# Negated copies of high weights, made on GpSimd instead of ScalarE

## The chip, the cores and the metric

The kernel runs on one core of one Trainium2 chip. The metric is the time of one execution in microseconds (us). Before the change it is 2362.22 us, the median of three runs (2359.66 to 2363.74).

## The reference

Two layers of a transformer-like trunk are computed for 128 context tokens and 512 latent tokens with shared weights of width 1024. Each layer is a half-step SwiGLU feed-forward block, a mixer (attention, pooling and convolution heads between an input and an output projection), and a second half-step feed-forward block. All are wrapped in modulated RMS norms:

```python
def ffn_sublayer(x, mod, k, g, w_in, w_out):
    h = modulated_norm(x, mod, k, g)
    gt, up = jnp.split(h @ w_in, 2, axis=-1)
    return x + 0.5 * mod[:, None, 3 * k + 2] * ((jax.nn.silu(gt) * up) @ w_out)

def trunk_layer(...):
    x = ffn_sublayer(x, mod, 0, norm_g[0], w_ffn_in[0], w_ffn_out[0])
    h = modulated_norm(x, mod, 1, norm_g[1])
    q, k, v, u_pool, u_conv, bg, cg = jnp.split(h @ w_in, IN_SPLITS, axis=-1)
    ...
    y = jnp.concatenate([attn, pool, conv], axis=-1) @ w_out
    x = x + mod[:, None, 5] * y
    x = ffn_sublayer(x, mod, 2, norm_g[2], w_ffn_in[1], w_ffn_out[1])
    return x, k, v
```

The modulation vectors come from a product of a condition vector with `w_ada` (1024 x 9216 for each layer). All data is float32.

## The kernel before

Activations are held transposed, features on the 128 partitions and 640 tokens along the row, in two halves of 320 columns. A float32 product is made from three faster ones (`mm3`, L352 to L354): every operand is split into a high part (rounded to float32r) and a low part (the rest), and the three matmuls are high weight by high activation, high weight by low activation, low weight by high activation. So each weight tile of 128 x 1024 passes four steps before TensorE can finish with it:

1. SyncE issues a load into a `raw` buffer (five of them; `load_raw`, L181).
2. ScalarE (ACT) copies it, rounded, into a `wh` buffer (four of them; L170).
3. The low part `wl` (four buffers) is made. Where `split_w` is given an engine, one subtraction on that engine does it (L176). Where it is not (`eng is None`), ScalarE writes the negated high part into `wl` (L173), and GpSimd (POOL) issues a DMA that adds `raw` onto `wl` (L174), so that `wl` becomes `raw - wh`.
4. TensorE (PE) multiplies; the third matmul of each triple (L354) reads `wl`.

A `raw` buffer is free for the next load only when its last reader is done, which in the second form of step 3 is the accumulating DMA. The loads of `w_ada` (L150) use the same five buffers in the first feed-forward block, where VectorE (DVE) multiplies and sums them (L309, L311).

The form without an engine is used 96 times: for all weights of the input product in the first feed-forward block but the first two columns (40), for all weights of the two mixers (44), and for the first four weights of each of the other three feed-forward blocks (12, `ups_by_half`). Most weights of those three blocks use sums of weight blocks (`fast_weights`) and the subtraction on VectorE.

At the end of each block `last_product` computes the last part of the output product half by half, and the residual stream `x` (L518), its squares (ScalarE, L251) and their sum (VectorE, L252) follow tile by tile. Then come the sum over partitions (PE, L375), the inverse root (L361 to L364) and the modulated norm: `norm_tail` (L401, L416, L417) ahead of a mixer, `seven` (L480, L483, L473, L474) ahead of a feed-forward block. While these run, the first four weights of the next block pass the steps above, because their `wh` buffers come free one after the other as `last_product` ends. These places are called transitions below; there are five, at about 523, 743, 1216, 1677 and 1900 us.

Each engine executes its instructions in the order of its own queue. That order is fixed when the program is built, by a list scheduler that goes by the order of the code and by durations that it assumes. An instruction that waits holds all that are behind it on its engine.

Of the kernel before, what the change touches and what calls it, by code (L numbers as in the profile page):

```python
# [12 lines left out]
AF = mybir.ActivationFunctionType  # L13
# [83 lines left out]
def trunk_kernel(ctx: ExitStack, tc: tile.TileContext, i: dict, o: dict):  # L97
    nc = tc.nc
# [21 lines left out]
    def f32(ap):  # L120
        return ap.bitcast(F32)
# [42 lines left out]
    def split_w(raw, nk, width, eng=None):  # L164

        view = lambda t: t[:, : nk * width].rearrange("p (k c) -> p k c", k=nk)
        size, tag = (1024, "") if nk * width > 512 else (512, "s")
        h = view(whp.tile([P, size], F32R, tag="wh" + tag, name="wh", bufs=4 if tag == "" else 2))
        lo = view(wlp.tile([P, size], F32R, tag="wl" + tag, name="wl", bufs=4 if tag == "" else 2))
        nc.scalar.activation(h, raw, AF.Copy)  # L170
        if eng is None:

            nc.scalar.activation(lo, f32(h), AF.Copy, scale=-1.0)  # L173
            nc.gpsimd.dma_start(lo, raw, accum_op=ALU.add)  # L174
        else:
            eng.tensor_tensor(lo, raw, f32(h), op=ALU.subtract)  # L176
        return h, lo
# [9 lines left out]
    def load_w(loads, nk=KD, width=P):  # L187
        return split_w(*raw_w(loads, nk, width))

    def load_cols(src, c0, width=P, eng=None):  # L190
        return split_w(*load_raw(src, c0, width), eng)
# [364 lines left out]
    def ffn(l, f, n, hs, side, finish, nxt, first=None):  # L556
# [83 lines left out]
        def fast_weights(j):  # L640

            nk = KD // 2
            up, *_ = load_raw(w_in, DFF + j * P)
            gate, *_ = load_raw(w_in, j * P)
            a1, a2, d1, d2 = up[:, :nk, :], up[:, nk:, :], gate[:, :nk, :], gate[:, nk:, :]
            add = lambda out, x, y: nc.vector.tensor_tensor(out, x, y, op=ALU.add)
            view = lambda t: t.rearrange("p (k c) -> p k c", k=KD)
            one, two = view(sum_tile()), view(sum_tile())
            ups = split_w(up, KD, P, nc.vector)
            add(one[:, :nk, :], a1, d1)  # L650
            add(one[:, nk:, :], d1, d2)
            add(two[:, :nk, :], one[:, nk:, :], a1)
            add(two[:, nk:, :], two[:, :nk, :], a2)
            late = split_w(d2, nk, P, nc.vector)
            twos = split_w(two, KD, P, nc.vector)
            ones = split_w(one, KD, P, nc.vector)
            first = lambda w: (w[0][:, :nk, :], w[1][:, :nk, :])
            second = lambda w: (w[0][:, nk:, :], w[1][:, nk:, :])
            return {1: first(ups), 2: second(ups), 3: second(twos), 4: late, 5: second(ones), 6: first(twos), 7: first(ones)}
# [731 lines left out]
```

## Time and profile before

| | us |
|---|---|
| median of three runs | 2362.22 |
| the profiled execution | 2360.58 |
| its span on the core | 2358.8 |
| PE busy | 2298.7 (97%) |
| DVE busy | 1546.5 (66%) |
| ACT busy | 1057.9 (45%) |
| POOL busy | 118.7 (5%) |

A row of the timeline gives the start, the duration, the engine, the line, the operation and its tiles, how many like it are merged into it, and in brackets how long the engine sat idle before it and what ended that. The chain of work that ended last is followed back from the last instruction, at each step to what released it. PEclk is the granted clock of TensorE as a share of full speed, and the DMA share is the mean busy share of 16 DMA engines.

### The profile page before, as it was taken

How to read it: one execution, taken by the hardware profiler on the slowest of the kernel's cores; microseconds unless marked ns; L12 is line 12 of the kernel's file. 1: busy time of each engine (PE TensorE's matmuls, PEld its weight loads, DVE VectorE, ACT ScalarE, POOL GpSimd, SP SyncE). 2: the span in 40 equal slices, each digit the busy share in tenths (PEclk: the TensorE clock that was granted, in tenths of full speed). 3: DMA queues.
4: the chain of work that ended last, by engine and by line, in shares of the span. 5: the costliest groups of instructions: out<-in, count | busy, mean ns of one | idle time of the engine just before them, and what ended most of it. 6: DMA issues, size and time to landing. Idle time of an engine off the chain costs nothing.

```text
span 2358.8 us, 40820 instructions
## 1 busy us (share of the span) xinstructions
PE 2298.7 (97%) x16558; PEld 2217.3 (94%) x16558; DVE 1546.5 (66%) x3166; ACT 1057.9 (45%) x1861; POOL 118.7 (5%) x151
## 2 busy tenths in 40 slices
PE   7899999999999999999999999999999999999999
PEld 6899999998978899999999999999898789999999
DVE  5546675556766766666669575676658687666674
ACT  4423232335766634243446343443556674344351
POOL 2101010001200000000000000000111000000000
PEclk9999999999999999999999999999999999999999
DMA  8858596727533444453433334433475232322321
GB/s 274 207 143 232 161 258 169 199 63 159 133 87 81 126 132 136 117 160 101 152 90 119 115 113 119 126 102 114 99 151 127 55 72 80 106 72 86 89 81 45
DMA packets 355124, 297.90 MB, mean 126 GB/s; under 512 B 27288, under 2 KB 303096, under 8 KB 354936
## 3 DMA queue, kind: packets, MB, share of 16 engines
q1 hardware_dynamic: 340932, 244.88, 34.4%
q0 software_dynamic: 13824, 50.34, 11.8%
q8 instruction: 130, 2.13, 0.4%
q14 instruction: 58, 0.48, 0.1%
q10 hardware_dynamic: 180, 0.07, 0.0%
HBM read 242.04 MB, written 2.88 MB: 104 GB/s over the span
## 4 chain that ended last, share of the span: by engine, by line
PE 82%; DMA 7%; DVE 4%; issue 4%; ACT 3%; ACTq 0%; POOL 0%; SPq 0%; POOLq 0%; DVEq 0%
PE acc L352 21%; PE acc L353 20%; PE acc L354 20%; PE mis L354 3%; PE mis L353 3%; PE mis L352 3%; DMA raw<-in_w_ffn_in 3%; DMA wl<-raw 2%; PE mis L275 2%; PE po L352 1%; PE po L353 1%; PE po L354 1%; PE po L1100 1%; PE acc L1060 1%; PE mis L1111 1%
## 5 line engine op out<-in xcount | busy, mean ns | idle before, releaser
L352 PE MATMUL acc<-h,wh 128*128 128x320 f32 (+1 forms) x2784 | 871.8, 315 | 22.6 <-ACT h L416 5.4
L353 PE MATMUL acc<-h,wh 128*128 128x320 f32 (+1 forms) x2784 | 865.7, 312 | 6.4 <-DVE h L412 3.9
L354 PE MATMUL acc<-h,wl 128*128 128x320 f32 (+1 forms) x2784 | 863.3, 311 | 8.3 <-DMA wl<-raw 8.3
L170 ACT ACTIVATE wh<-raw 128x1024 fp32r<-128x1024 f32 (+2 forms) x332 | 305.1, 920 | 624.8 <-PE mis L353 287.6
L352 PEld LDWEIGHTS acc<-h,wh 128*128 128x128 f32 x2784 | 527.0, 190 | 38.5 <-issue 12.0
L354 PEld LDWEIGHTS acc<-h,wl 128*128 128x128 f32 x2784 | 527.4, 190 | 11.6 <-DMA wl<-raw 11.2
L353 PEld LDWEIGHTS acc<-h,wh 128*128 128x128 f32 x2784 | 527.7, 190 | 8.6 <-DVE h L412 4.1
L176 DVE TENSOR_TENSOR wl<-raw,wh 128x1024 fp32r<-128x1024 f32 (+2 forms) x234 | 227.8, 974 | 53.4 <-ACT wh L170 48.9
L352 PE MATMUL acc<-g,wh 128*128 128x320 f32 x832 | 258.2, 310 | 0.0
L353 PE MATMUL acc<-g,wh 128*128 128x320 f32 x832 | 258.0, 310 | 0.0
L354 PE MATMUL acc<-g,wl 128*128 128x320 f32 x832 | 257.3, 309 | 0.0
L170 ACT ACTIVATE wh<-sums 128x1024 fp32r<-128x1024 f32 x120 | 126.4, 1059 | 204.6 <-PE acc L353 93.0
L176 DVE TENSOR_TENSOR wl<-sums,wh 128x1024 fp32r<-128x1024 f32 x120 | 146.4, 1224 | 70.4 <-ACT wh L170 51.0
L518 DVE SCALAR_TENSOR_TENSOR x<-acc,gate,x 128x128 f32<-128x128 f32 (+1 forms) x352 | 125.2, 393 | 84.1 <-PE acc L354 82.5
L353 PE MATMUL mis<-g,wh 128*128 128x320 f32 x576 | 177.9, 309 | 0.0
L354 PE MATMUL mis<-g,wl 128*128 128x320 f32 x576 | 177.8, 309 | 0.0
L352 PE MATMUL mis<-g,wh 128*128 128x320 f32 x576 | 177.8, 309 | 0.0
L174 POOL DMA_DIRECT2D wl<-raw x96 | 84.3, 878 | 1714.3 <-DVE x L518 1030.9
L352 PEld LDWEIGHTS acc<-g,wh 128*128 128x128 f32 x832 | 156.3, 188 | 1.8 <-issue 1.6
L354 PEld LDWEIGHTS acc<-g,wl 128*128 128x128 f32 x832 | 156.4, 188 | 0.2
L353 PEld LDWEIGHTS acc<-g,wh 128*128 128x128 f32 x832 | 156.3, 188 | 0.3
L311 DVE SCALAR_TENSOR_TENSOR sums<-raw,c,sums 128x512 f32<-128x512 f32 x196 | 135.1, 744 | 27.5 <-DMA raw<-in_w_ada 27.4
(208 smaller groups left out, 3206.5 us busy)
## 6 DMA issues: line engine op xcount, KB each, us to landing
raw<-in_w_ffn_in SPq DMA_DIRECT2D x176, 512.0 KB, 4.3
raw<-in_w_ada SPq DMA_DIRECT2D x128, 512.0 KB, 5.8
wl<-raw POOLq DMA_DIRECT2D x96, 512.0 KB, 5.6
raw<-in_w_ffn_out SPq DMA_DIRECT2D x48, 512.0 KB, 4.8
raw<-in_w_ffn_out SPq DMA_DIRECT2D x64, 320.0 KB, 3.7
raw<-in_w_in SPq DMA_DIRECT2D x20, 512.0 KB, 5.4
adaw<-in_w_ada SPq DMA_DIRECT2D x16, 512.0 KB, 10.1
raw<-in_w_in SPq DMA_DIRECT2D x16, 256.0 KB, 6.5
```

Of the source, the lines that this page charges most:

```text
L170: nc.scalar.activation(h, raw, AF.Copy)
L174: nc.gpsimd.dma_start(lo, raw, accum_op=ALU.add)
L176: eng.tensor_tensor(lo, raw, f32(h), op=ALU.subtract)
L275: last = nc.tensor.matmul(ps[32 * g : 32 * g + 32, 0:P], c2[:, 2 * q + k, :], r[:, k, g * P : (g + 1) * P], start=(q + k == 0), stop=(q + ...
L311: nc.vector.scalar_tensor_tensor(part[:, j, :], r[:, k, :], c, part[:, j, :], op0=ALU.mult, op1=ALU.add)
L352: nc.tensor.matmul(out, wh, xh, start=start, stop=False, skip_group_check=onto)
L353: nc.tensor.matmul(out, wh, xl, start=False, stop=False, skip_group_check=onto)
L354: return nc.tensor.matmul(out, wl, xh, start=False, stop=stop, skip_group_check=onto)
L518: nc.vector.scalar_tensor_tensor(xT[t][:, s:e], ps[:, s - a : e - a], gates[l][n][:, t, j : j + 1], xT[t][:, s:e], op0=ALU.mult, op1=ALU.add,)
L1060: nc.tensor.matmul(ps[:, :w], qs[2 * c + m][:, g, self.qc], self.kk[x][:, g, :], start=(x == 0), stop=(x == 1),)
L1100: nc.tensor.matmul(po[g * HD : (g + 1) * HD, 0:256], self.vs[x][:, g * HD : (g + 1) * HD], pts[:, g * 256 : (g + 1) * 256], start=(x == 0) ...
L1111: nc.tensor.transpose(pt[:, (g * 2 + m) * P : (g * 2 + m + 1) * P], self.pr[m][:, g, x * P : (x + 1) * P], ident,)
```

## The change

In the form without an engine, the negated copy of the high part is made by GpSimd, with a multiplication of the tile by -1, and not by ScalarE. GpSimd then issues the accumulating DMA as before. All 96 uses change alike. Nothing else is edited.

```diff
         nc.scalar.activation(h, raw, AF.Copy)
         if eng is None:
 
-            nc.scalar.activation(lo, f32(h), AF.Copy, scale=-1.0)
+            nc.gpsimd.tensor_scalar_mul(lo, f32(h), -1.0)
             nc.gpsimd.dma_start(lo, raw, accum_op=ALU.add)
         else:
             eng.tensor_tensor(lo, raw, f32(h), op=ALU.subtract)
```

## Rows read from the trace of the kernel before

**Rows 1.** The page: span, and busy time, share and instructions by engine.

```profile
span 2358.8 us, 40820 instructions
PE 2298.7 (97%) x16558; PEld 2217.3 (94%) x16558; DVE 1546.5 (66%) x3166; ACT 1057.9 (45%) x1861; POOL 118.7 (5%) x151
```

**Rows 2.** The page: chain that ended last, shares of the span by engine.

```profile
PE 82%; DMA 7%; DVE 4%; issue 4%; ACT 3%; ACTq 0%; POOL 0%; SPq 0%; POOLq 0%; DVEq 0%
```

**Rows 3.** Waits of PE: who waited for whom, us in total, times, longest.

```profile
PE acc L354 <- DMA wl<-raw: 8.3, 9, 1.7
```

**Rows 4.** Groups of instructions by form: busy us, mean ns | idle before, releasers.

```profile
L173 ACT ACTIVATE wl<-wh 128x1024 fp32r<-128x1024 f32 x96 | 101.2, 1056 | 1.0
L176 POOL TENSOR_TENSOR wl<-raw,wh 128x1024 fp32r<-128x1024 f32 x2 | 4.8, 2404 | 18.9 <-ACT wh L170 18.9
```

**Rows 5.** Timeline of POOL: six memsets in a run.

```profile
534.01 3.96 POOL L853 MEMSET pool<- 128x672 f32 x6
```

**Rows 6.** Timelines of ACT, POOL and PE, 59 to 70 us.

```profile
59.67 1.06 ACT L170 ACTIVATE wh<-raw 128x1024 fp32r<-128x1024 f32 x1 [3.93 <-PE acc L353]
63.11 1.04 ACT L173 ACTIVATE wl<-wh 128x1024 fp32r<-128x1024 f32 x1
64.75 1.01 POOL L174 DMA_DIRECT2D wl<-raw  x1 [13.49 <-ACT g L155]
69.48 0.56 PE L354 MATMUL acc<-h,wl 128*128 128x320 f32 x2 [1.71 <-DMA wl<-raw]
```

**Rows 7.** Timelines of ACT, POOL and PE, 76 to 117 us.

```profile
76.15 1.06 ACT L170 ACTIVATE wh<-raw 128x1024 fp32r<-128x1024 f32 x1 [3.82 <-PE acc L353]
79.50 0.87 POOL L174 DMA_DIRECT2D wl<-raw  x1 [5.92 <-ACT wl L173]
95.65 1.06 ACT L170 ACTIVATE wh<-raw 128x1024 fp32r<-128x1024 f32 x1 [3.04 <-DMA raw<-in_w_ffn_in]
100.12 0.86 POOL L174 DMA_DIRECT2D wl<-raw  x1 [14.08 <-ACT wl L173]
116.96 0.64 PE L352 MATMUL acc<-h,wh 128*128 128x320 f32 x1 [3.30 <-ACT sg L585]
```

**Rows 8.** The chain that ended last, one piece of 56 to 125 us.

```profile
113.38 2.74 DVE sums L311 x4
```

**Rows 9.** Busy time by stretch: PE, PEld, DVE, ACT, POOL; then PEclk, DMA share, GB/s.

```profile
74.00:84.00 10.00, 10.00 (x70) 10.00 (x69) 1.02 (x4) 4.30 (x7) 0.87 (x1) 1.00 1.06 255
...
118.00:120.00 2.00, 2.00 (x9) 2.00 (x8) 0.00 (x0) 1.97 (x3) 0.87 (x1) 0.50 0.61 183
```

**Rows 10.** Timelines of ACT, POOL and PE, the transition at 1216 us.

```profile
1221.24 1.04 ACT L170 ACTIVATE wh<-raw 128x1024 fp32r<-128x1024 f32 x1
1224.47 1.04 ACT L173 ACTIVATE wl<-wh 128x1024 fp32r<-128x1024 f32 x1
1225.92 0.89 POOL L174 DMA_DIRECT2D wl<-raw  x1 [4.76 <-DVE full L480]
1240.05 0.41 PE L353 MATMUL acc<-h,wh 128*128 128x320 f32 x1 [1.90 <-DVE h L474]
```

**Rows 11.** Timelines of ACT and POOL, the transition at 523 us.

```profile
530.50 1.06 ACT L170 ACTIVATE wh<-raw 128x1024 fp32r<-128x1024 f32 x1 [0.56 <-PE acc L353]
533.27 0.86 POOL L174 DMA_DIRECT2D wl<-raw  x1 [2.66 <-ACT wl L173]
```

**Rows 12.** Timeline of ACT, the transition at 743 us.

```profile
767.51 0.63 ACT L170 ACTIVATE wh<-raw 128x512 fp32r<-128x512 f32 x1 [5.67 <-DMA raw<-in_w_ffn_in]
```

**Rows 13.** Timeline of DVE beside POOL subtractions, then beside POOL memsets.

```profile
19.76 6.64 DVE L401 SCALAR_TENSOR_TENSOR tmp<-x,gain,rr 128x128 f32<-128x128 f32 x8
...
536.35 0.93 DVE L401 SCALAR_TENSOR_TENSOR tmp<-x,gain,t 128x128 f32<-128x128 f32 x3
```

**Rows 14.** Busy time by stretch, the transition at 743 us.

```profile
743.00:760.00 17.00, 15.80 (x105) 15.07 (x103) 14.07 (x33) 16.15 (x31) 3.16 (x4) 1.00 0.61 125
```

## The prediction

> **What bounds the kernel now.** The page comes first: PE is busy for 2298.7 of 2358.8 us [rows 1], and the chain that ended last runs over PE for 82% [rows 2]. ACT, which the change relieves, is busy 45% of the span, so its busy time as a sum is worth nothing. Only the some 60 us in which PE does not work can shrink or grow, and the time at which its clock is low. So the second view is PE's waits: the third matmul of a triple waits for the accumulated low weights in nine places, 8.3 us together and 1.7 us at most [rows 3]. All nine lie between 60 and 120 us or in the five transitions; from 123 us to the end of that block, and through the long middle of the other blocks, PE hardly waits. So the change is worth what it does in these six places, and the third reading is the timelines there: when `wh` of a weight ends on ACT, when its accumulating DMA starts on POOL, and who waits for that.
>
> **What is removed and added.** ACT loses 96 copies of 1.056 us, 101 us in all [rows 4], POOL gains 96 multiplications. POOL has 118.7 us of work [rows 1] and waits most of the time, so its sum is no limit; the duration of one counts, since it stands in the path of each weight. No row shows a one-input multiplication of 128 x 1024 on POOL. From below: six memsets of 672 columns, which only write, take 3.96 us, 0.66 each [rows 5]; by columns that is 1.0 us for 1024. From above: the subtraction of the same size, which reads two tiles, takes 2.4 us [rows 4]. If writing costs 1.0, each of the two reads costs 0.7, and one read gives 1.0 (hidden under the write) to 1.7 (added to it). I take 1.3, nearer the memset, and keep 1.0 and 2.4 as ends. The Trainium skill ("GPSIMD Engine Reference", section 4.1 Engine selection) calls GpSimd roughly at line rate for one-input elementwise work; with its clock of 1.2 GHz that is, as an estimate, 0.85 us. By that alone the sum below would be 2 to 3 us better; no row before shows it.
>
> **The gap from `wh` to the DMA.** Where nothing disturbs it, the path is the end of `wh`, 1.06 us of copy, then 0.4 us from ACT to POOL (1224.47 + 1.04 to 1225.92 [rows 10]): 1.5 us at best. At 530.50 + 1.06 to 533.27 it is 1.7 [rows 11]. After the change it is the same hop of 0.4, 1.3 of multiplication, and a hand-over to the DMA behind it on POOL, which no row shows and I put at 0.2 (0 to 0.4): 1.9 us. So an undisturbed weight loses 0.2 to 0.4 us. But on ACT the copy stands in a queue with other work, and there the gap is much longer. POOL has next to nothing else to do. So the gain lies where the gap of before is well above 1.9.
>
> **Place 1, 60 to 123 us.** Three links follow one another on the chain that ended last. (a) `wh` ends at 60.73 and the copy starts only at 63.11, behind a table load and the activations of the two columns before; the DMA starts at 64.75 and PE waits for it until 69.48 [rows 6]. Gap 4.0, after it 1.9: 2.1 us earlier. The activations that stood behind the copy move up by 1 us as well, so the next `wh`, for which PE also waits, is no later than that. (b) `wh` ends at 77.21, DMA at 79.50 [rows 7]: 2.3 to 1.9, 0.4 earlier. Its landing frees a `raw` buffer for the load whose arrival starts the `wh` at 95.65. (c) That ends at 96.71, its DMA starts at 100.12 [rows 7], since activations that waited for DVE stood between: 3.4 to 1.9, 1.5 earlier. Its landing frees the buffer for a load of `w_ada`, for which DVE's sums at 113.38 wait [rows 8]; behind them stand the bias copies, then the activation that frees PSUM, and PE waits 3.30 us until 116.96 [rows 7]. Sum 4.0 us. SP issues these loads in its own order behind the DMAs' landings, so its queue moves with them. After that wait TensorE runs at 0.50 (1.2 GHz): 9 matmuls in 2 us where 70 in 10 us are usual [rows 9]. That lasts from 117 to some 122.4 us, 5.4 us at 4.5 in place of 7 matmuls per us, a loss of 2 us. The wait would shrink to some 1.4 us (3.30 less the 1.9 by which the end of the chain gains on PE), and I expect the clock to stay up: 2 us more. From there PE is busy without a break, so what is won stays.
>
> **Place 2, transition at 1216 us.** `wh` ends at 1222.28, the DMA starts at 1225.92, since five other pieces of ACT stood before the copy [rows 10]: 3.6 to 1.9, 1.7 us. This DMA frees the buffer for a load for which DVE's in-order queue waits with the norm behind it, up to PE's wait until 1240.05 [rows 10]. Gain 1.7 us.
>
> **The other four transitions.** The gap that decides is the 1.7 of [rows 11] or within 0.1 of it: 0.2 us later each, 0.8 us lost.
>
> **DVE.** The new instruction can hold DVE. Beside the two subtractions on POOL, eight DVE instructions took 6.64 us, 0.83 each; beside POOL's memsets three of the same shape took 0.93, 0.31 each [rows 13]. So POOL work that reads held DVE for 4 of its 4.8 us, work that only writes did not. The multiplication reads one tile. The ends are no hold and 1.3 us each. In the transition at 743 us DVE is idle for 2.9 of 17 us [rows 14], so four holds (5.2 us) push it by up to 2.3 us; but there ACT waits 5.67 us for a load behind all this [rows 12], which covers it. In the two transitions to a mixer a hold of the last addition of squares (up to 0.9 us) ends before the last low weights land. So I charge nothing for it, with up to 4 us (two uncovered pushes) kept for the range. The Trainium skill ("SBUF — State Buffer", section "Who interferes with whom") says that a VectorE instruction with two SBUF inputs contends with any GpSimd instruction that reads SBUF, and names no exception for one input: by it the full hold applies, which speaks against this change. The rows agree as far as they go. By the rule the 4 us are possible; without a hold the sum stays as it is.
>
> **The sum.** 4.0 + 2.0 + 1.7 - 0.8 = 6.9 us. The profiled execution took 2360.58 us, 1.8 more than its span, and becomes 2353.7. The median of the runs is 1.6 above it, so I predict 2355.
>
> **The rivals.** (R1) The waits close only partly. Between 74 and 84 us the DMA share is 1.06 [rows 9], and an earlier DMA into full queues may land no earlier. Then links b and c and the clock are lost and 2.1 + 1.7 - 0.8 = 3.0 remain: 2359 for the median, within 0.2%. For it speaks the share, against it that link c runs over queues and hand-overs, not bytes. (R2) Slower, by the multiplication itself. At its upper end of 2.4 us the gap is 3.0. Link a keeps 1.0, b loses 0.7, c keeps 0.4, 1216 keeps 0.6: 1.3 won, without the clock. The other four transitions lose 1.3 each, 5.2. Four holds are now 9.6 us against 2.9 idle at 743, 1.0 more than the 5.67 us of cover, and 1216 and 1900 are alike, 3 in all. Net 7 us slower: 2369. The gains and these prices balance near 1.9 us for one multiplication; from some 2.2 on it is slower by more than 0.2%. For it speaks the subtraction's 2.4, against it that only one tile is read. (R3) The build orders the queues anew. The scheduler goes by assumed durations, so an instruction may come to stand elsewhere. One bad place costs like the one at 767.51, 5.67 us on ACT [rows 12], of which PE sees 3 to 5; one good place gives as much. No row can say which. It widens the range on both sides.
>
> **How the numbers follow.** A measurement of this kernel can tell about 0.2%, 4.7 us, from no change. Forecast 0.50 (faster, 2355; with multiplications of 1.0 us, and the rest of the waits for low weights gone, down to 2347). R1 0.28, at 2359. R2 0.10, at 2369. R3 0.12, split evenly into 0.04 each for faster, same and slower. The uncovered holds move 0.02 from the forecast's faster to slower. Faster 0.50 + 0.04 - 0.02 = 0.52; same 0.28 + 0.04 = 0.32; slower 0.10 + 0.04 + 0.02 = 0.16. The range takes in the forecast's lower end and R1 with some loss, and reaches to just under R2: 2347 to 2368.
>
> **What would show it right or wrong.** Right: multiplications near 1.3 us on POOL, starting some 0.4 us behind `wh`; the DMA of link a near 62.6 us, that of link c some 4 us earlier; PE's wait near 117 us under 2 us and PEclk at full there; the wait near 1240 us earlier; nothing changed from 123 to 520 us but the shift. Wrong: multiplications of 2 us and more, DVE instructions of twice their length beside them, longer waits of PE for `wl` or for squares in the transitions, or another order of the queues with a new wait.

## The result and the profile after

The change makes the kernel slower: 2404.1 us (median of 4 runs, 2401.1 to 2405.72) against 2360.94 us for the kernel before on the same chip (4 runs), a ratio of 1.0177 with a 95% interval of 1.016 to 1.0194. The forecast was 2355, its range ended at 2368. The profiled execution has a span of 2403.9 us, against 2358.8 [rows 1].

The page after, with busy time by engine, then the chain that ended last by engine:

```profile
PE 2312.9 (96%) x16558; PEld 2229.9 (93%) x16558; DVE 1600.5 (67%) x3166; ACT 967.9 (40%) x1765; POOL 399.7 (17%) x247
PE 70%; issue 7%; DMA 5%; POOL 3%; DVE 2%; ACT 2%; SPq 0%; ACTq 0%; POOLq 0%; DVEq 0%
```

ACT lost 90 us and POOL gained 281, as the change says. But DVE, which the diff does not touch, gained 54 us with the same 3166 instructions, and POOL has come onto the chain. The other shares of the chain can't be laid beside [rows 2]: after the change it is followed back only to 255 us, and it opens there with 51 us of "issue", while the shares are still of the whole span. PE is busy for 14.2 us longer with the same 16558 matmuls: TensorE's granted clock is 0.983 in the mean of this execution, where it was 0.993. So some of the 45 us between the two spans are not waits but matmuls at the lower clock.

The costliest groups after, by form (busy us, mean ns | idle before and releasers): the new multiplication, the subtraction with two inputs beside it, and three groups of DVE whose code is unchanged.

```profile
L173 POOL TENSOR_SCALAR wl<-wh 128x1024 fp32r<-128x1024 f32 x96 | 286.1, 2980 | 1457.5 <-ACT wh L170 1429.2 <-ACT pts L1117 24.6 <-DMA out_new_k<-ko 3.7
L176 POOL TENSOR_TENSOR wl<-raw,wh 128x1024 fp32r<-128x1024 f32 x2 | 4.8, 2404 | 18.2 <-ACT wh L170 18.2
L252 DVE TENSOR_TENSOR ssq<-ssq,sq 128x320 f32<-128x320 f32 x70 | 45.2, 646 | 21.4 <-ACT sq L251 20.7
L309 DVE TENSOR_SCALAR sums<-raw,c 128x512 f32<-128x512 f32 x28 | 23.7, 872 | 14.4 <-DMA raw<-in_w_ada 14.3
L932 DVE TENSOR_TENSOR qw<-rope 128x512 f32<-128x512 f32 x8 | 9.4, 1177 | 0.6
```

One multiplication takes 2.98 us in the mean (2.76 to 5.76 over the 96, median 2.79). That is longer than the subtraction that reads two tiles, 2.40 here as in [rows 4], which the forecast had taken as its upper end. The three DVE groups had means of 489, 480 and 691 ns before.

Waits of PE after (us in total, times, longest):

```profile
PE acc L352 <- ACT h L473: 12.2, 4, 5.7
PE mis L375 <- DVE ssq L252: 9.5, 2, 4.8
PE acc L352 <- ACT sg L585: 8.2, 7, 2.7
PE acc L1060 <- DVE mx L1071: 7.4, 2, 4.2
PE acc L354 <- DMA wl<-raw: 6.5, 3, 4.4
PE acc L352 <- DVE u L1026: 5.5, 2, 2.8
```

The wait for the accumulated low weights, on which the forecast was built (8.3 us [rows 3]), has shrunk a little in total and is longer in its worst place. The loss is in other rows: norms and squares at the transitions, activations in the first block, the attention's scores. So the question is by which way a longer step on POOL reaches them, and where.

For that the two traces were laid over each other: the start of the n-th matmul of one kernel, less the start of the n-th matmul of the kernel before, at four marks (in us of the kernel before). The stretch to 135 us holds the forecast's place 1; the attention starts are 611 to 705 and 1759 to 1853 us. Each number is what a kernel lost (or won, negative) in that stretch, from one profiled execution each; the experiments of the next section stand in the same table. Single executions of the kernel before lie between 2355.0 and 2365.2 us, so a difference of 2 us in one stretch can be chance.

| kernel | to 135 | 135 to 513, rest of the first block | the two attention starts | all other | last matmul |
|---|---|---|---|---|---|
| after the change | -2.1 | 12.9 | 19.0 | 15.4 | 45.2 |
| e1, extra reads on POOL | -2.2 | 4.9 | 20.4 | 6.3 | 29.4 |
| e2, delay only | 1.8 | 7.3 | 2.4 | 6.5 | 18.0 |
| e5, POOL busy without reads | -0.4 | 6.3 | 2.7 | 1.7 | 10.3 |
| e6, a longer delay | 5.3 | 17.2 | 9.9 | 5.1 | 37.5 |
| e3, subtraction on POOL | -3.9 | 1.3 | 20.4 | 15.5 | 33.3 |
| e9, half on POOL, half on ACT | -2.4 | 0.7 | 13.6 | 9.6 | 21.5 |
| e4, change in the first block alone | -3.5 | 13.1 | 0.5 | -3.5 | 6.6 |
| e7, e3 in the first block alone | -6.1 | 1.3 | 1.1 | -1.0 | -4.7 |
| e8, subtraction on DVE there | -11.1 | -0.9 | 2.5 | 0.9 | -8.6 |
| e10, subtraction on DVE everywhere | -10.8 | -0.9 | 12.5 | -0.5 | 0.3 |

### The profile page after: what moved, and what is told of

It is laid out like the page before. It is cut to its first block, busy times and chain, and to the rows that moved or that the text cites. A ratio compares the mean times of both kernels' runs of the same rounds, so it can differ in the third digit from the quotient of the medians.

```text
span 2403.9 us, 40815 instructions
## 1 busy us (share of the span) xinstructions
PE 2312.9 (96%) x16558; PEld 2229.9 (93%) x16558; DVE 1600.5 (67%) x3166; ACT 967.9 (40%) x1765; POOL 399.7 (17%) x247
## 4 chain that ended last, share of the span: by engine, by line
PE 70%; issue 7%; DMA 5%; POOL 3%; DVE 2%; ACT 2%; SPq 0%; ACTq 0%; POOLq 0%; DVEq 0%
PE acc L352 18%; PE acc L354 17%; PE acc L353 17%; PE mis L354 3%; PE mis L353 3%; PE mis L352 3%; DMA raw<-in_w_ffn_in 3%; POOL wl L173 2%; DMA wl<-raw 2%; PE mis L275 1%; PE po L353 1%; PE po L354 1%; PE po L352 1%; PE po L1100 1%; PE acc L1060 1%
## 5 line engine op out<-in xcount | busy, mean ns | idle before, releaser
L352 PE MATMUL acc<-h,wh 128*128 128x320 f32 (+1 forms) x2784 | 875.2, 317 | 33.5 <-ACT h L473 12.2
L170 ACT ACTIVATE wh<-raw 128x1024 fp32r<-128x1024 f32 (+2 forms) x332 | 305.1, 919 | 668.4 <-PE mis L353 289.6
L173 POOL TENSOR_SCALAR wl<-wh 128x1024 fp32r<-128x1024 f32 x96 | 286.1, 2980 | 1457.5 <-ACT wh L170 1429.2
L170 ACT ACTIVATE wh<-sums 128x1024 fp32r<-128x1024 f32 x120 | 126.0, 1058 | 200.7 <-PE acc L353 91.8
```

The costliest lines, as they stand in the source:

```text
L173: nc.gpsimd.tensor_scalar_mul(lo, f32(h), -1.0)
L352: nc.tensor.matmul(out, wh, xh, start=start, stop=False, skip_group_check=onto)
```

## The experiments

Three theories stood at the start. T1: the way to the low weight is longer, so what waits for it, or for the `raw` buffer that it frees, comes later. T2: POOL's reads hold DVE. T3: the scheduler put the queues in another order, which costs by itself. A fourth, T4, came with the first results: POOL is busy for longer with each weight, so that the next weight's transfer waits in its queue.

To size T1, one figure is taken from each trace: for each of the 96 uses, the time from the end of ACT's activation that makes `wh` (L170) to the start of POOL's issue of the accumulating DMA (L174). Its median is 1.72 us before and 3.38 us after the change.

**e1, reads without a delay.** POOL does the reading beside the weight's own path.

```diff
             nc.scalar.activation(lo, f32(h), AF.Copy, scale=-1.0)
-            nc.gpsimd.dma_start(lo, raw, accum_op=ALU.add)
+            extra_negations(nc, tc, idle, f32(h), nc.gpsimd.dma_start(lo, raw, accum_op=ALU.add))
+def extra_negations(nc, tc, idle, h, last):
+    flat = h.rearrange("p k c -> p (k c)")
+    for c in (0, 480):
+        with tc.issue_after(last.ins):
+            last = nc.gpsimd.tensor_scalar_mul(idle, flat[:, c : c + 480], -1.0)
```

> The copy stays on ACT, as before; behind each accumulating transfer GpSimd makes two more multiplications of 480 columns of the same high weight into a scratch tile that nobody uses. The result is the same. So GpSimd reads about as much per weight (960 of 1024 columns, about 2.6 us by the 2.79 us that 1024 columns took after the change), but no low weight waits for these reads, unless the next weight's transfer is queued behind them. Theory T1 (the longer way to the low weight: 2.8 us instead of 1.06 us and a hand-over): between 2360 and 2372 us. Theory T2 (GpSimd's reads hold DVE): DVE's busy time goes up by about 45 us as it did after the change, and the time is 2385 us or more, most of the 43 us. Theory T3 (another order of the queues): 2360 to 2365 us, since the copy is where it was.

Measured: 2389.45 us, ratio 1.0118 (1.0094 to 1.0142), 28.8 us above before. DVE was busy for 1611.3 us. That is T2's number, for reads that nobody needs, with the copy where it was before. T3 has no part in it: in the trace of e1 the instructions of PE, DVE and ACT and the loads stand in the order of before. But the gap from `wh` to the DMA also grew a little, to 2.35 us, since a DMA can stand behind the extra reads; e5 takes that apart.

**e2, a delay without reads.** The fills write a scratch tile and read nothing; `seen` ties them behind ACT's copy.

```diff
-            nc.scalar.activation(lo, f32(h), AF.Copy, scale=-1.0)
-            nc.gpsimd.dma_start(lo, raw, accum_op=ALU.add)
+            seen = small.tile([P, 1], F32, tag="seen", name="seen", bufs=4); nc.scalar.activation(lo, f32(h), AF.Copy, scale=-1.0, accum_out=seen)
+            delayed(nc, tc, idle, seen, lambda: nc.gpsimd.dma_start(lo, raw, accum_op=ALU.add))
+def delayed(nc, tc, idle, seen, issue):
+    pause = nc.gpsimd.memset(seen, 0.0)
+    for _ in range(4):
+        ...
+            pause = nc.gpsimd.memset(idle, 0.0)
```

> The copy stays on ACT; between its end and the issue of the accumulating transfer GpSimd makes five fills of a scratch tile (one of 1 column, four of 200), which write and read nothing. By the fills in the trace of before this is about 1.8 us per weight; the result is the same. T1 (the longer way to the low weight): DVE's busy time stays within 10 us of before's 1546 us and the time is 2385 to 2405 us. T2 (reads hold DVE): 2361 to 2370 us. T3 (order): 2361 to 2365 us.

Measured: 2377.92 us, ratio 1.0068 (1.0048 to 1.0088), 17.3 us above before; DVE 1549.0 us, as before. The median gap is 3.29 us, nearly the 3.38 of the changed kernel, so this is about the price of the change's delay with DVE left free (425 matmuls, nearly all at the transitions, also come in another order). It lies between what T1 and T2 expected, so neither alone explains the change at the price that was put on it.

**e3, the shortest way on POOL.** One subtraction in place of copy and accumulating DMA.

```diff
-            nc.scalar.activation(lo, f32(h), AF.Copy, scale=-1.0)
-            nc.gpsimd.dma_start(lo, raw, accum_op=ALU.add)
+            nc.gpsimd.tensor_tensor(lo, raw, f32(h), op=ALU.subtract)
```

> The low weight is made by one subtraction on GpSimd, raw minus high, of 2.4 us; copy and accumulating transfer are both left out, the result is the same up to rounding. The low weight is ready 2.4 us and a hand-over after the high one, where it was about 8 us before and about 10 us after the change. T1 (the longer way): 2345 to 2362 us, no slower than before. T2 (reads hold DVE; here both operands are read, for 2.4 us per weight): DVE's busy time at least 35 us above before's, the time 2380 us or more, though the way to the low weight is the shortest of all. T3: not told apart.

Measured: 2396.2 us, ratio 1.0148 (1.0123 to 1.0173), as T2 expected. DVE was busy for 1677.7 us, 131 more than before. The table shows where each theory holds: in the first block, where the delay counted, the kernel is ahead (-3.9) or hardly behind (1.3); at the attention starts it loses 20.4 us, though its low weights are ready 2.4 us behind the high ones, where the adding transfer alone took 5.6 at the median before.

**e4, the change in the first block alone.**

```diff
+            (nc.gpsimd.tensor_scalar_mul(lo, f32(h), -1.0) if on_pool[0] else nc.scalar.activation(lo, f32(h), AF.Copy, scale=-1.0))
...
+        last = x == len(steps) - 1; on_pool[0] = x == 0
```

> The multiplication is on GpSimd in the first feed-forward block alone (40 of the 96 uses) and on ACT in the rest. By the drift of the matmul starts between the two traces the change had lost 10.8 us by the end of that block (2.1 won to 134 us, 12.9 lost from there): T1 and T2 both expect 2369 to 2374 us. T3 (the order of the whole program is rebuilt and costs by itself): the loss isn't where the edit is, so less than 5 us or more than 20 us.

Measured: 2370.95 us, ratio 1.0046 (1.0031 to 1.0061), 10.3 us above before, as expected from the drift. The loss of 13.1 us lies in the stretch where the edit is, and behind it nothing is lost. That is against T3, but not all of it, since the queues of the later blocks are those of before in e4. The order can be read from the traces: after the change 48 matmuls between 60 and 80 us and 500 at the transitions behind 705 us stand elsewhere than before, and none in the rest of the first block or at the attention starts. So PE's order does not explain the losses there. DVE's order is another in the first block, at 46 places behind 135 us; in e9 it is another at 29, with 0.7 us lost. What the new order costs at the transitions, inside the 15.4 us of "all other", no run shows.

**e5 and e6, POOL busy or late, without reads.** e5 is e1 with ten fills in place of the two reads; e6 is e2 with eight fills in place of four.

```diff
-            nc.gpsimd.dma_start(lo, raw, accum_op=ALU.add)
+            pauses(nc, tc, idle, nc.gpsimd.dma_start(lo, raw, accum_op=ALU.add), 10)
+def pauses(nc, tc, idle, last, n):
+    for _ in range(n):
+        with tc.issue_after(last.ins):
+            last = nc.gpsimd.memset(idle, 0.0)
```

> As in the run with extra reads, the copy stays on ACT and GpSimd is kept busy behind each accumulating transfer, but by ten fills of a scratch tile (200 columns, 0.28 us and 0.04 us between them in the run with the delay: 3.2 us), which read nothing. GpSimd's time per weight is then that of the run with extra reads (3.26 us behind a transfer of 0.92 us); the result is the same. If the 28.8 us of that run came from reads that hold DVE (T2): DVE stays within 10 us of before's 1546 us and the time is 2361 to 2368 us. If they came from GpSimd's queue being long (a theory T4: the next weight's transfer, and the loads behind it, start later): 2380 us or more.

Measured: 2369.73 us, ratio 1.0033 (1.002 to 1.0045), 9.4 us above before, just over what T2 alone expected and far from T4's 2380.

> As in the run with the delay, but with eight fills instead of four between ACT's copy and the transfer: about 2.7 us, the length of the multiplication in the changed kernel, with nothing read; the result is the same. The way to the low weight and GpSimd's time per weight are then both those of the changed kernel or a little longer, and only DVE is free. If delay and hold add up, and the delay is worth what is left of the 43 us (about 14 to 18 us for the 1.3 us of the earlier run, more here): 2380 to 2395 us. If the delay alone explains the change: 2400 us or more. If it were worth nothing beyond the earlier run: 2378 us.

Measured: 2396.78 us, ratio 1.0157 (1.0141 to 1.0174), 36.4 us above before, 1.8 over the range that was given. The delay turned out longer than meant: the median gap is 5.04 us, since ACT's 1.06 us stand ahead of the fills. So e6 overshoots the change's own delay and can't be compared with it directly. It gives a slope: 36.4 us for 3.32 us of delay, 11.0 us for each; e2 has 17.3 for 1.57, the same 11.0. POOL's longer queue is in both.

e1 against e5 is the clean pair for the reads. First e1, then e5: busy time, POOL's extra instructions, and the DVE group that shows it best.

```profile
PE 2310.3 (97%) x16558; PEld 2225.6 (93%) x16558; DVE 1611.3 (67%) x3166; ACT 1060.4 (44%) x1861; POOL 406.0 (17%) x343
L1397 POOL TENSOR_SCALAR idle<-wh 128x480 bf16<-128x480 f32 x192 | 312.9, 1629 | 7.9
L932 DVE TENSOR_TENSOR qw<-rope 128x512 f32<-128x512 f32 x8 | 7.5, 937 | 0.6
```

```profile
PE 2306.7 (97%) x16558; PEld 2222.8 (94%) x16558; DVE 1550.8 (65%) x3166; ACT 1057.3 (45%) x1861; POOL 378.7 (16%) x1111
L1396 POOL MEMSET idle<- 128x200 f32 x960 | 292.1, 304 | 49.6
L932 DVE TENSOR_TENSOR qw<-rope 128x512 f32<-128x512 f32 x8 | 5.5, 690 | 0.6
```

POOL spends as long per weight in both (3.3 and 3.6 us with the idle time between), and the gap from `wh` to the DMA is 2.35 and 2.25 us. What differs is the reads (and the number of instructions, two for ten), and they cost 19.7 us (2389.45 less 2369.73); the order of the queues is that of before in e5 too. With reads, L932 takes 937 ns in the mean; with fills 690, as before. By the table, 17.7 us of that lie at the attention starts (20.4 less 2.7).

So the experiments price three parts of the change: 17.3 us for the delay (e2), 9.4 for POOL's longer queue (e5), 19.7 for the held DVE (e1 less e5). They add to 46.4 where 43.2 were measured. They need not add exactly, since e2 has some of the longer queue in it and a hold beside a wait is hidden; e1 also held DVE for longer than the change does (60.5 us more busy time than e5, where the change has 54.0 more than before). Each part was measured in another kernel, so its size within the changed kernel is an estimate. By the table e1 and e2 together give 12.2 us in the rest of the first block, 22.8 at the attention starts and 12.8 elsewhere, where the change lost 12.9, 19.0 and 15.4.

**e7 and e8, the other way to the low weight, in the first block alone.** A subtraction in place of copy and accumulating DMA, for those 40 weights: on POOL in e7 (`nc.gpsimd`), on DVE in e8.

```diff
+        eng = eng or first[0]
...
+        last = x == len(steps) - 1; first[0] = nc.vector if x == 0 else None
```

> The low weight by one subtraction on GpSimd, without copy and accumulating transfer, in the first feed-forward block alone (40 of 96 uses); the rest as before. By the drift of the run that did it everywhere (2.6 us ahead of before at 513 us of before's time, all losses behind it): 2355 to 2360 us. A theory by which any hold of DVE costs where it happens: 2370 us or more.

> The same subtraction in the first block alone, but on DVE: about 1.1 us per weight of DVE's own time (two SBUF inputs, 1024 columns, by the 0.49 us for 320 and 0.74 us for 512 columns: up to 1.5 us), against 2.5 us that GpSimd's held it. If in this block the way to the low weight is what counts: 2353 to 2360 us. If DVE has no room there: 2365 us or more.

Measured: e7 2358.57 us, ratio 0.9997 (0.9987 to 1.0006), no difference, though DVE was busy for 57.9 us more (1604.4). So a hold does not cost its full length wherever it happens; the shorter way may hide some of its cost. e8 2352.39 us, ratio 0.9969 (0.9959 to 0.998), faster than both kernels, 0.6 below its range. DVE's subtraction took 1.22 us, and the 45 us of work that DVE gained (1591.8 for 1546.5 us) found room there. The same window of before and of e8 shows what was to be won (PE, PEld, DVE, ACT, POOL busy; then PEclk, DMA share, GB/s):

```profile
60.00:134.00 74.00, 65.83 (x427) 64.35 (x429) 31.64 (x68) 33.45 (x52) 9.67 (x11) 0.95 0.83 206
```

```profile
60.00:134.00 74.00, 74.00 (x513) 73.60 (x512) 54.87 (x101) 26.54 (x47) 0.00 (x0) 1.00 0.53 150
```

PE is never idle in e8 and its clock is at 1.00 (2.4 GHz) in the mean of the window, so 8.2 us of idle time and the slow stretches are both gone: 11.1 us by the drift.

**e9, the multiplication at the length that the forecast assumed.** POOL takes 512 columns, ACT the other 512.

```diff
-            nc.scalar.activation(lo, f32(h), AF.Copy, scale=-1.0)
+            (m := nk // 2, nc.scalar.activation(lo[:, m:], f32(h)[:, m:], AF.Copy, scale=-1.0), nc.gpsimd.tensor_scalar_mul(lo[:, :m], f32(h)[:, :m], -1.0))
```

> Each negated copy is shared: 512 of its 1024 columns on GpSimd (about 1.4 us by the 2.79 us of 1024), 512 on ACT (about 0.55 us), at the same time; the accumulating transfer follows both. The result is the same. So GpSimd's multiplication has about the length that the forecast assumed (1.3 us) and the transfer starts about as early after the high weight as before (1.5 to 1.9 us). By the forecast's own sum: 2351 to 2358 us. By the parts measured since (17.3 us for a transfer 1.6 us later, 9.4 us for GpSimd's queue at 3.2 us more per weight, 19.4 us for 3.3 us of reads): a transfer about 0.2 us later 2 us, queue 3 to 4 us, reads 8 to 9 us, so 2370 to 2378 us.

Measured: 2380.38 us, ratio 1.0086 (1.0071 to 1.0101), 20.6 us above before, 2.4 over the range of the parts and 22 over the forecast's sum. The multiplication took 1.48 us at the median, the gap 2.05. Of the 6.0 us that the forecast put on place 1 it won 2.4, with 0.7 lost in the rest of that block; at the attention starts, which the forecast left out, 13.6 us were lost.

**e10, subtraction on DVE for all 96.** `first[0]` is `nc.vector` throughout.

> The low weight by one subtraction on DVE (1.1 to 1.2 us) in all 96 uses, without copy and accumulating transfer. In the first block alone this brought the time to 2352 us. If DVE's own time is what the other places lack (at the attention starts and the changes between blocks PE waits for DVE), the 56 more uses cost more than they bring: 2356 to 2372 us. If the length of the way counts there too: 2345 to 2352 us.

Measured: 2356.39 us, ratio 0.999 (0.998 to 0.9999), no difference that counts. The 11 us of the first block come again and 12.5 us go at the attention starts, where PE waits for DVE (its wait for `u`, L1026, is 8.0 us in place of 1.3). That agrees with T2: there DVE's time seems to be short, whether its own work or a hold takes it. But 50 matmuls of each attention start also come in another order.

## Why the prediction failed, step by step

**What bounds the kernel.** That PE is the bound, and that only its waits and its clock can move, was right. The step that failed is "so the change is worth what it does in these six places". A stretch in which PE hardly waits was read as one in which there is slack. In the rest of the first block, where the forecast expected "nothing changed from 123 to 520 us but the shift", 12.9 us were lost. Pieces of the chain that ended last, after, from that stretch (start, us, what):

```profile
306.88 3.94 POOL wl L173
311.23 5.26 DMA wl<-raw
316.53 5.74 DMA raw<-in_w_ada
322.37 0.76 DVE sums L311
...
325.72 8.97 DMA raw<-in_w_ffn_in
334.80 1.06 ACT wh L170
```

The multiplication, 3.94 us long here, delays the landing, the landing frees a `raw` buffer, SP's queue stands for that buffer with the load of `w_ada` and the load of a weight behind it, and that weight's `wh` comes late. The forecast followed this very loop as link c, but only where PE already waited.

**The multiplication (1.3 us, bounds 1.0 and 2.4).** The term of the sum that was mis-sized: 2.79 at the median, above the upper end. Both steps behind it failed: that a read adds less than a write, and that one input can't take longer than two. The Trainium skill ("GPSIMD Engine Reference", section 4.1 Engine selection) calls one-input work roughly line-rate, which was estimated at 0.85 us; here it took more than three times that, and the measurement decides.

**The gap (1.9 us).** Timelines of ACT, POOL and PE after, 59 to 70 us, for link a:

```profile
59.04 1.06 ACT L170 ACTIVATE wh<-raw 128x1024 fp32r<-128x1024 f32 x1 [3.93 <-PE acc L353]
60.19 2.79 POOL L173 TENSOR_SCALAR wl<-wh 128x1024 fp32r<-128x1024 f32 x1 [9.57 <-ACT wh L170]
63.31 1.04 POOL L174 DMA_DIRECT2D wl<-raw  x1 [0.33 <-POOL wl L173]
68.08 0.64 PE L354 MATMUL acc<-h,wl 128*128 128x320 f32 x1 [3.27 <-DVE g L156]
```

The hop from ACT to POOL took 0.1, not 0.4, and the hand-over to the DMA 0.33, not 0.2; with 2.79 between them the gap is 3.2 us. Against 4.0 before [rows 6] link a kept 0.8 of its 2.1. Links b (78.75 to 81.97) and c (94.48 to 97.70) have the same 3.2: against 2.3 and 3.4 before [rows 7], b lost 0.9 and c won 0.2. That is nothing in sum. PE still waited, 3.27 us at 68 us (the DVE instruction named ended at 66.2; a transfer issued at 63.31 that takes 4.6 to 5.3, as in the chain above and below, lands then).

**Place 1 and the clock.** The kernel was 2.1 us ahead at 135 us all the same. This is no merit of the shorter path: e1, which keeps the copy on ACT and the order of all queues, is 2.2 ahead there too. e4, with the same edit in this place, is 3.5 ahead. Whether any of it is more than chance is not shown. The clock did not stay up; its slow stretches moved (windows after, columns as above):

```profile
68.00:72.00 4.00, 3.92 (x15) 3.92 (x16) 1.84 (x2) 0.96 (x2) 3.70 (x3) 0.50 0.85 138
100.00:110.00 10.00, 8.23 (x47) 8.24 (x48) 8.53 (x18) 2.97 (x6) 6.41 (x2) 0.83 0.91 264
```

At 68 to 72 us PE works at 1.2 GHz after a stretch with the wait of 3.27 us, as it did at 118 us before [rows 9] after a wait of 3.30 us [rows 7]. That this place holds a gain was right (6.0 with the clock were forecast, e8 won 11.1). It took a way to the low weight without a transfer.

**Transition at 1216 us (1.7 won).** Lost instead: 4.4 us between 1171 and 1341 us. A new wait of 4.39 us for a low weight stands there, and the chain of one weight after the other on POOL is behind it: 2.8 to 3.1 us of multiplication and 0.9 of issue give about 4 us per weight, four weights in a row.

```profile
1244.92 2.77 POOL L173 TENSOR_SCALAR wl<-wh 128x1024 fp32r<-128x1024 f32 x1 [458.70 <-ACT wh L170]
1248.09 0.90 POOL L174 DMA_DIRECT2D wl<-raw  x1 [0.41 <-DVE full L480]
1249.41 2.76 POOL L173 TENSOR_SCALAR wl<-wh 128x1024 fp32r<-128x1024 f32 x1 [0.42 <-ACT wh L170]
1252.58 0.92 POOL L174 DMA_DIRECT2D wl<-raw  x1 [0.41 <-POOL wl L173]
1259.58 0.64 PE L354 MATMUL acc<-h,wl 128*128 128x320 f32 x1 [4.39 <-DMA wl<-raw]
```

The forecast had called POOL free, "next to nothing else to do"; with one weight behind the other POOL's own next multiplication is what else it has to do.

**DVE (nothing charged, 4 us kept).** The second failed step, and by the prices above the larger. The hold exists, near the size that the forecast wrote down as an end (1.3 us) and then covered. Timelines of POOL, DVE and PE after, the first transition to a mixer:

```profile
536.44 1.37 DVE L252 TENSOR_TENSOR ssq<-ssq,sq 128x320 f32<-128x320 f32 x1 [0.81 <-ACT sq L251]
540.23 3.12 POOL L173 TENSOR_SCALAR wl<-wh 128x1024 fp32r<-128x1024 f32 x1
540.42 1.55 DVE L252 TENSOR_TENSOR ssq<-ssq,sq 128x320 f32<-128x320 f32 x1 [0.60 <-ACT sq L251]
543.03 0.49 DVE L252 TENSOR_TENSOR ssq<-ssq,sq 128x320 f32<-128x320 f32 x1 [0.60 <-ACT sq L251]
544.58 1.54 DVE L252 TENSOR_TENSOR ssq<-ssq,sq 128x320 f32<-128x320 f32 x1 [0.60 <-ACT sq L251]
546.17 1.43 PE L375 MATMUL mis<-ssq,ones 128*128 128x320 f32 x2 [4.83 <-DVE ssq L252]
```

An addition of squares that starts beside a multiplication takes 1.37 to 1.55 in place of 0.49 us. Three are held here, 3.0 us in all, and PE's wait for the squares is 4.83 us where it was 1.88; the forecast had let one hold of up to 0.9 us end in time. And it looked for holds only at the transitions. 44 of the 96 uses are in the mixers, and by e1 less e5 nearly all of the holds' cost (17.7 of 19.7 us) is at the attention starts. There PE has two long waits after the change, and only the first is a hold's. DVE and POOL work on the queries in turn, one after the other. The last addition of a query (L932), before and after, and PE's wait:

```profile
634.01 0.69 DVE L932 TENSOR_TENSOR qw<-rope 128x512 f32<-128x512 f32 x1
...
648.72 1.34 DVE L932 TENSOR_TENSOR qw<-rope 128x512 f32<-128x512 f32 x1
663.10 0.42 PE L352 MATMUL acc<-mix,wh 128*128 128x320 f32 x1 [2.82 <-DVE u L1026]
```

Held for 0.65 us, it makes the time from one query to the next 9.43 us where it was 8.86 (8.8 in e2 and e5, which read nothing). The products `u` stand behind the queries, and PE waits 2.82 us for them, 0.7 at most before. e1 has this wait at 3.97 us.

In the second wait DVE is not held but idle, for the load of the masks. POOL before and after, then after's chain, DVE and PE:

```profile
640.91 1.30 POOL L930 TENSOR_TENSOR rope<-qw,turn 128x512 f32<-128x512 f32 x1 [5.72 <-DVE qw L918]
642.16 0.88 POOL L174 DMA_DIRECT2D wl<-raw  x1
...
656.20 1.30 POOL L930 TENSOR_TENSOR rope<-qw,turn 128x512 f32<-128x512 f32 x1 [3.64 <-DVE qw L918]
657.49 3.29 POOL L173 TENSOR_SCALAR wl<-wh 128x1024 fp32r<-128x1024 f32 x1
661.18 4.60 DMA wl<-raw
...
667.20 6.97 DMA masks<-in_masks
674.32 0.56 DVE L1071 CUSTOM_DVE_ANT_0 pr<-acc,masks 128x384 f32<-128x384 f32 x1 [4.83 <-DMA masks<-in_masks]
674.93 0.69 PE L1060 MATMUL acc<-kh,q 128*128 128x384 f32 x1 [3.25 <-DVE mx L1071]
```

POOL's part of a query (L930) stands ahead of the multiplication in POOL's queue. Before, ACT had made the copy by then, and the transfer was issued 1.25 us after L930 began; now it is 4.98 us. The loads behind it on SP, and the masks at their end, come later with it. e6, which reads nothing, has this wait of PE too (3.07 us), and e1 has not. So at the attention starts the changed kernel pays for the delay as well, and how its 19.0 us divide between hold and delay is not shown. Some of them are the clock's, to which the forecast looked in place 1 alone. The first attention start before and after (columns as above):

```profile
611.00:705.00 94.00, 92.11 (x601) 80.31 (x600) 71.64 (x216) 60.46 (x137) 12.17 (x12) 1.00 0.46 106
...
625.00:728.00 103.00, 95.50 (x603) 83.57 (x602) 74.83 (x216) 53.01 (x129) 36.83 (x21) 0.97 0.43 96
```

PE is idle for 7.5 in place of 1.9 us, and busy for 3.4 us longer with about as many matmuls, at a granted clock of 0.97 in the mean.

The Trainium skill ("SBUF — State Buffer", section "Who interferes with whom") had it right that a DVE instruction with two SBUF inputs contends with a GpSimd instruction that reads SBUF, and not with one that only writes it: L932, an addition of two SBUF tiles, shows both halves in e1 and e5 (937 and 690 ns).

**The rivals.** R2 came, with its mechanism in part. Its price for the multiplication was 12.7 us for each microsecond (2355 at 1.3, 2369 at 2.4); e2 and e6 give 11.0 for each microsecond of delay. That the two are near is luck: its places were wrong, transitions in place of the first block, and its balance point of 1.9 us too high: e9 with 1.48 us is slower by 20.6 already, mostly at the attention starts. At 2.79 us R2's own line gives 2374; the 30 us from there to 2404 are near what e1 and e5 measured for holds and POOL's queue (29.1), but R2 has 3 us of holds in it already. R1 is refuted by the result. R3 finds no support in the rest of the first block and at the attention starts, where PE's order is that of before; its share at the transitions stays open.

## What to carry to other kernels

That an engine waits most of the time says that its sum is free, not that its latency is: before a step is moved to it, walk the loop from that step through the buffer that it frees back to the loads, also where the bound engine does not wait today. Ask which engine the new one disturbs, over all places where the moved instruction runs, and charge the hold where that engine has no idle time. Where a step stands on the path, taking it out (one subtraction in place of a copy and an adding transfer, on the engine with time to spare in that stage) was worth more than moving it.

## What the runs showed of the hardware

- A one-input multiplication on POOL (128 x 1024, float32 in, float32r out) took 2.79 us at the median, longer than the two-input subtraction of that size (2.40 at the median in e3). 512 columns took 1.48.
- The hold of a two-input addition on DVE ended before the multiplication did. The one at 540.23 us runs to 543.35, but the DVE instruction beside its start is through at 541.97, and the one at 543.03 takes its usual 0.49 us. The rule of the Trainium skill ("SBUF — State Buffer", section "Who interferes with whom") that one side keeps the shared ports for its whole instruction, stated there for DVE's faster modes, does not describe these additions. It was not so for every instruction: an L309, with one tile as input, that began 1.79 us into the multiplication at 132.85 us ended at 135.90, 0.28 us behind its end. So one length of the hold for all cases does not come out of the trace.
- The hold goes both ways. The longest multiplication, 5.76 us, began beside eight sums of `w_ada` on DVE (timelines of DVE and POOL after):

```profile
100.92 5.38 DVE L311 SCALAR_TENSOR_TENSOR sums<-raw,c,sums 128x512 f32<-128x512 f32 x8
103.17 5.76 POOL L173 TENSOR_SCALAR wl<-wh 128x1024 fp32r<-128x1024 f32 x1 [4.58 <-ACT wh L170]
```

- A DVE instruction with one tile as input was held as well: L309 took 872 ns in place of 480, and 505 in e5, where POOL only writes.
